# Expert weights of a mixture-of-experts block streamed into a mix of 8 KB and 4 KB slots, with four more tiles of on-chip memory

## The chip, the cores and the metric

The kernel runs on one core of a Trainium2 chip. The metric is the device time of one execution in microseconds; of several executions the median counts. A profile of one further execution, with its own time, shows what each engine did.

## What is computed

One decoder layer on 256 tokens of 1024 channels: four token mixers, merged by gates, then a mixture of 32 experts, each with 256 hidden channels, with a normalisation after either half. The change touches the second half, of which this is the core:

```python
def one_seq(xs):                      # xs: 256 x 1024
    lg = (xs @ wr_g) + br_g           # 4 groups, the best one is taken
    ...                               # two of its eight experts, weights in gate (256 x 32)
    hg = jnp.einsum('sd,edh->seh', xs, w_gate)   # w_gate, w_up: 32 x 1024 x 256
    hu = jnp.einsum('sd,edh->seh', xs, w_up)
    h = jax.nn.silu(hg) * hu * gate[..., None]
    return jnp.einsum('seh,ehd->sd', h, w_down)  # w_down: 32 x 256 x 1024
```

The weights of one expert are three matrices of 1 MiB, so all experts together are 96 MiB. Every expert's weights are read, whichever tokens chose it.

## The kernel before, in words

**The two halves.** The token mixers run first. Their work is written as generators (`gen_S`, `gen_P`, `gen_D` and so on), and the string `ORDER` says, letter by letter, which of them goes on next; so each engine's order of work is written out by hand. The mixers' weights come as loads of 512 KiB (128 partitions with 1024 floats each) into tiles of the pool `rp`, which has `NW` = 35 such tiles. Mixer activations share these tiles.

**The experts' weights.** The list `stream` (L1219) holds all expert loads in the order of use. Experts are worked on in eight groups of four. For each group there are 8 loads of `mwg` (the gate matrices), 8 of `mwu` (up) and 8 of `mwd` (down); each is half of one expert's matrix, 512 KiB, and for each matrix the first halves of all four experts stand ahead of the second halves. The down matrices of the last two groups come last. `fetch()` (L1229) takes the next load of the list, takes a tile for it and issues the DMA on SP's queue. Of 46 loads in a row, 13 go to tiles of the pool `rb` (`NR`, opened when the mixers' own memory is given back) and 33 to tiles of `rp` (`NF`). The letter `L` in `ORDER` calls `fetch()` 46 times (`NL`) while the mixers still run. After that `wload()` (L1253) calls it for each tile that is needed; since SP has its own queue, a load goes out as soon as the tile that it reuses is free and SP has come to it. SP issues in order: a load that waits holds back all loads behind it. Every load also waits until the load eight places ahead of it on SP has landed, since eight semaphores are used in turn.

**The work on a group** (loop at L1518). `gather` (L1429) picks the tokens of the four experts by a matrix product. For `mwg`, then for `mwu`, the loop at L1523 goes over the eight blocks of 128 channels and, inside, over the four experts; each product has 32 columns, and the four experts take four separate column groups of the array (L1527). A product of float32 runs in two passes, so 32 products are 64 rows of the trace. Then follow the activation (L1547 to L1549), two transposes (L1552), the down products (L1496), and `back` (L1514), which adds the result to the tokens. For the last two groups the down products stand behind the loop (L1617 on); their last eight 512 KiB loads are issued as sixteen halves (L1242), and `last_back` (L1642), the statistics and the output follow.

The loop for more tokens than an expert has room for (L1683 on) is not entered with these inputs.

Of the kernel before, what the change touches and what calls it, by code (L numbers as in the profile page):

```python
# [9 lines left out]
F32 = mybir.dt.float32  # L10
# [103 lines left out]
def _layout(inp):  # L114
    g = {k: np.asarray(v) for k, v in inp.items()}
    x = g["x"][0]
    W = g["w_in"][0]
    f = np.float32
    o = {}
# [23 lines left out]
    o["win"] = np.stack(cols)  # L143
    o["wbr"] = g["w_branch"][0].reshape(4, 2, P, 2, 512).transpose(0, 3, 2, 1, 4)
    o["wout"] = g["w_out"][0].reshape(KT, P, D)
    o["mwg"] = g["moe_w_gate"][0].reshape(NEXP, 2, 4, P, HID).transpose(0, 1, 3, 2, 4)
    o["mwu"] = g["moe_w_up"][0].reshape(NEXP, 2, 4, P, HID).transpose(0, 1, 3, 2, 4)
    o["mwd"] = g["moe_w_down"][0].reshape(NEXP, 2, P, D)
    pc = np.zeros((P, NPC), f)

    def put(name, a):
# [21 lines left out]
    for h in range(4):  # L173
        j = 64 * (h % 2)
# [21 lines left out]
MID = 8  # L196
NEAR = 6

NW = 35
NR = 13  # L200
NF = 33
N2 = 19
N1 = 10
NL = 46
RB = 0
LATE = 2
WARM = 5
# [7 lines left out]
    "ADDSAAADDAAABAAAABADDDDBDDDBBDDBBPDBBSDBSBBBBBBDDPDDBBBPCBCBPCSBBCBASPCLCMMCCCCCDMNCMCMCPCCSCCNCPSCP"  # L215
    "PSCPMMNPSPSMPCNMMMCCCDMNPPMSMPSMPSNPMCXLLMLLLLLLLPSPSPSPMPSPPSLPNNMLLMLLLSPMSLMLPSPLPSMPSPMNNPMLPSPS"
    "MMMPSMPSMNNMMMLMMPLMPSPSUMMPMMPMUUSUMUPMMUMPMMMPOUOLMLLLLMLULLUOULLLULMOUULULLMOUUOUUOQOQLQQQQQQQQLQ"
    "QYYLQQUQQQQORLOLLLRLRQRRLRQRRQRRRRQRRRZQZQERRRRRRRLRREQEEQRRE"
)


def body(ctx, tc, I, out):
    nc = tc.nc
    V, A, G, T, SY = nc.vector, nc.scalar, nc.gpsimd, nc.tensor, nc.sync
# [5 lines left out]
    rp = ctx.enter_context(tc.tile_pool(name="rp", bufs=NW))  # L230

    def view(t, n, shape):
        t = t[0:shape[0], 0:n]
        if len(shape) == 2:
            return t
        d = "abcde"[:len(shape) - 1]
        return t.rearrange("p (%s) -> p %s" % (" ".join(d), " ".join(d)), **dict(zip(d, shape[1:])))

    def slot(name, shape, pool=None, dt=F32):

        t = (pool or rp).tile([P, 1024], dt, tag="w", name=name)
        return view(t, int(np.prod(shape[1:])), shape)
# [963 lines left out]
    MP = {}  # L1206
# [12 lines left out]
    stream = []  # L1219
    for g in range(NQUAD + 1):  # L1220
        if g < NQUAD:
            stream += [(src, (4 * g + e, kh), [P, 4, HID]) for src in ("mwg", "mwu") for kh in range(2) for e in range(4)]

        if g != NQUAD - 2:
            for j in ((NQUAD - 2, NQUAD - 1) if g == NQUAD else (g,) if g < NQUAD - 2 else ()):
                stream += [("mwd", (4 * j + e, k), [P, D]) for k in range(2) for e in range(4)]
    fetched, tails = [], []

    def fetch():  # L1229
        n = len(fetched)  # L1230
        src, (e, k), shape = stream[n]
        t = slot("w", shape, MP["rb"] if RB <= n % (NR + NF) < RB + NR else rp)
        fetched.append(t)
        if n < len(stream) - 8:
            SY.dma_start(t, I[src][e][k])
            return

        tails.append((t, I[src][e][k]))
        if n == len(stream) - 1:
            for hs in (slice(0, 512), slice(512, 1024)):  # L1240
                for t, a in tails:
                    SY.dma_start(t[:, hs], a[:, hs])  # L1242
# [245 lines left out]
    outs, wds = {}, {}  # L1488

    def downs(g):  # L1490
        wds[g] = [[wload() for _ in range(4)] for k in range(2)]
        return [ps([P, 512], pj) for _ in range(2)]

    def down(g, k, h, pd):
        for e4 in range(4):
            T.matmul(pd[h][32 * e4:32 * e4 + 32], lhsT=outs[g][0][:, k, 32 * e4:32 * e4 + 32], rhs=wds[g][k][e4][:, 512 * h:512 * h + 512],  # L1496
                     start=k == 0, stop=k == 1, tile_position=(0, 32 * e4))

    def small(shape):
# [18 lines left out]
    for g in range(NQUAD):  # L1518
        xg = XG.pop(g)
        weights(g)  # L1520
        more = g + 1 < NQUAD
        pgu = ps([P, 2, HID])
        for i, src in enumerate(("mwg", "mwu")):  # L1523
            ws = [[wload() for _ in range(4)] for kh in range(2)]
            for k in range(KT):
                for e4 in range(4):
                    T.matmul(pgu[32 * e4:32 * e4 + 32, i], lhsT=xg[:, k, 32 * e4:32 * e4 + 32], rhs=ws[k // 4][e4][:, k % 4, :],  # L1527
                             start=k == 0, stop=k == KT - 1, tile_position=(0, 32 * e4))
            if i == 0:
# [38 lines left out]
        if g < NQUAD - 2:  # L1568
            pd = downs(g)
# [65 lines left out]
    g = NQUAD - 1  # L1635
# [15 lines left out]
    pd = downs(g)  # L1651
# [31 lines left out]
    with tc.If(flag > 0):  # L1683
# [13 lines left out]
        with tc.For_i(0, NEXP, 1) as e:  # L1697
            wg, wu, wd_ = ([slot("wo", sh) for _ in range(2)] for sh in ([P, 4, HID], [P, 4, HID], [P, D]))
            for i in range(2):
                SY.dma_start(wg[i], I["mwg"][bass.ds(e, 1)][0, i])  # L1700
                SY.dma_start(wu[i], I["mwu"][bass.ds(e, 1)][0, i])
                SY.dma_start(wd_[i], I["mwd"][bass.ds(e, 1)][0, i])
            hx = slot("hx", [P, 2, S])
            pg = ps([P, 2, S])
            pu2 = ps([P, 2, S])
# [42 lines left out]
```

## Time and profile before

| | |
|---|---|
| median of 3 executions | 513.37 us (512.88 to 514.83) |
| the profiled execution, its own time | 511.94 us |
| its span, first to last instruction | 510.2 us |
| mean granted TensorE clock | 0.981 |
| PE busy | 467.2 us (92%) |
| DVE, ACT, POOL busy | 241.7, 195.8, 47.0 us |
| moved by DMA | 146.82 MB |

The profiled execution took 1.7 us more than its span; it is 1.4 us under the median. "Busy" counts the time in which at least one instruction of the engine was under way. PE is TensorE, PEld its weight loads, DVE VectorE, ACT ScalarE, POOL GpSimd, SP the engine that issues DMAs. Idle time is put down to what ended it. The span can be read in three stretches: the mixers until about 290 us, the routing of tokens until 299.5 us, and the experts from there on.

### The profile page before, as it was taken

Reading aid. Unit: us, or ns where it says so; the run is one execution under the profiler, and the core shown is the slowest. Engines: PE = TensorE matmul, PEld = TensorE weight load, DVE = VectorE, ACT = ScalarE, POOL = GpSimd, SP = SyncE. Lnnn points to the kernel's source line nnn. Section 1 sums busy time; section 2 is a strip of 40 time slices with the busy share of each in tenths; the row PEclk is TensorE's granted clock in tenths of the full one; section 3 lists DMA queues with packets and bytes.
Section 4 is the critical chain, followed back from the end, with each engine's and each line's share of the span. In section 5 each row is a group of like instructions: output and inputs, shape, how many; then the busy total and the mean of one; then the engine's idle time right before and its main releaser. Section 6 shows DMA issues by size and latency. Waiting matters only on the chain. (4 is left out here: it accounts for less than half of the span.)

```text
span 510.2 us, 10633 instructions
## 1 busy us (share of the span) xinstructions
PE 467.2 (92%) x4396; PEld 357.0 (70%) x4396; DVE 241.7 (47%) x479; ACT 195.8 (38%) x357; POOL 47.0 (9%) x55
## 2 busy tenths in 40 slices
PE   8999999999999999999999899998898989777891
PEld 6888887998778999999998676554453635343420
DVE  4786659987868558544764643021111211111015
ACT  5967555366494465434353342020201201001311
POOL 2003022300000012123150000000000000000002
PEclk9999999999999999999999989999999999989896
DMA  8999432212332452999879869999999999999962
GB/s 283 350 371 383 141 110 84 89 39 84 123 127 84 145 187 90 408 410 409 336 288 413 287 242 406 407 409 408 409 408 408 409 409 409 408 410 408 401 239 84
DMA packets 44410, 146.82 MB, mean 288 GB/s; under 512 B 4996, under 2 KB 7624, under 8 KB 44360
## 3 DMA queue, kind: packets, MB, share of 16 engines
q1 hardware_dynamic: 44360, 146.12, 75.0%
q8 instruction: 35, 0.57, 0.4%
q14 instruction: 15, 0.12, 0.1%
HBM read 143.48 MB, written 2.62 MB: 286 GB/s over the span
## 5 line engine op out<-in xcount | busy, mean ns | idle before, releaser
L374 PE MATMUL ps<-xl,hi 128*128 128x256 f32 x416 | 122.3, 294 | 1.9 <-DVE vS L385 1.1
L375 PE MATMUL ps<-xh,lo 128*128 128x256 f32 x416 | 118.0, 284 | 0.4 <-DVE lo L360 0.3
L376 PE MATMUL ps<-xh,hi 128*128 128x256 f32 x416 | 117.6, 283 | 0.0
L360 DVE TENSOR_TENSOR lo<-w,hi 128x1024 fp32r<-128x1024 f32 (+1 forms) x75 | 89.1, 1206 | 53.1 <-ACT hi L359 45.5
L374 PEld LDWEIGHTS ps<-xl,hi 128*128 128x128 f32 x416 | 79.7, 192 | 5.6 <-issue 1.9
L375 PEld LDWEIGHTS ps<-xh,lo 128*128 128x128 f32 x416 | 79.7, 192 | 2.6 <-issue 1.4
L359 ACT CAST hi<-w 128x1024 fp32r<-128x1024 f32 (+1 forms) x75 | 74.2, 1014 | 16.9 <-PE ps L375 5.1
L376 PEld LDWEIGHTS ps<-xh,hi 128*128 128x128 f32 x416 | 79.7, 192 | 0.0
L1527 PE MATMUL ps<-w,xg 128*32 128x256 f32 x1024 | 69.0, 393 | 7.8 <-DMA w<-mwu 7.0
L1527 PEld LDWEIGHTS ps<-w,xg 128*32 128x32 f32 x1024 | 34.0, 112 | 39.7 <-DMA w<-mwu 12.2
L1429 PE MATMUL ps<-Sel,nrm 128*128 128x128 f32 x256 | 33.6, 286 | 1.3 <-DVE smr L1395 0.7
L1429 PEld LDWEIGHTS ps<-Sel,nrm 128*128 128x128 f32 x256 | 31.3, 200 | 4.8 <-issue 4.1
L1514 PE MATMUL ps<-small,SGT 128*128 128x512 f32 x48 | 23.7, 616 | 9.1 <-DVE small L1508 5.1
L1508 DVE COPY small<-ps 128x512 f32<-128x512 f32 x6 | 4.2, 692 | 53.2 <-PE ps L1514 53.2
L1479 ACT COPY SGT<-ps 128x256 f32<-128x256 f32 x8 | 3.0, 373 | 65.8 <-PE ps L1477 65.8
L1496 PE MATMUL ps<-w,small 128*32 128x512 f32 x192 | 24.7, 599 | 3.7 <-ACT xg L1436 3.0
L1514 PEld LDWEIGHTS ps<-small,SGT 128*128 128x128 f32 x48 | 8.2, 189 | 24.9 <-DVE small L1508 10.1
L1669 POOL TENSOR_TENSOR res<-res,ln 128x512 f32<-128x512 f32 x1 | 1.7, 1730 | 239.2 <-ACT res L1668 239.2
L1422 DVE TENSOR_TENSOR Sel<-rank,csts 128x128 f32<-128x128 f32 x16 | 4.0, 288 | 32.7 <-PE ps L1477 32.7
L374 PE MATMUL ps<-parts,hi 128*128 128x256 f32 x64 | 18.8, 293 | 0.0
L1496 PEld LDWEIGHTS ps<-w,small 128*32 128x32 f32 x192 | 5.4, 109 | 18.3 <-ACT xg L1436 7.5
L375 PE MATMUL ps<-parts,lo 128*128 128x256 f32 x64 | 18.1, 283 | 0.0
(417 smaller groups left out, 703.2 us busy)
## 6 DMA issues: line engine op xcount, KB each, us to landing
w<-mwg SPq DMA_DIRECT2D x64, 512.0 KB, 10.2
w<-mwu SPq DMA_DIRECT2D x64, 512.0 KB, 10.2
w<-mwd SPq DMA_DIRECT2D x56, 512.0 KB, 10.2
w<-win SPq DMA_DIRECT2D x54, 512.0 KB, 5.4
w<-wbr SPq DMA_DIRECT2D x8, 512.0 KB, 4.1
w<-wout SPq DMA_DIRECT2D x8, 512.0 KB, 7.9
w<-mwd SPq DMA_DIRECT2D x16, 256.0 KB, 5.3
scr<-fsb SPq DMA_DIRECT2D x1, 1536.0 KB, 7.0
```

The lines of the kernel that those rows point to most:

```text
L359: A.copy(hi, src)
L360: V.tensor_tensor(lo, src, hi.bitcast(F32), op=OP.subtract)
L374: T.matmul(dst, lhsT=ls[0], rhs=rs[1], start=start, stop=False)
L375: T.matmul(dst, lhsT=ls[1], rhs=rs[0], start=False, stop=False)
L376: T.matmul(dst, lhsT=ls[0], rhs=rs[0], start=False, stop=stop)
L1422: V.tensor_tensor(t, rank[q][:, 4 * g:4 * g + 4, None].broadcast_to([P, 4, 32]), C("iota")[:, None, :].broadcast_to([P, 4, 32]), op=OP.is_ ...
L1429: T.matmul(pg[:, k4], lhsT=nrm[q][:, 128 * k:128 * k + 128], rhs=f2(SelR[g, q]), start=q == 0 and k4 == 0, stop=True, skip_group_check=True)
L1479: A.copy(SGT, pg)
L1496: T.matmul(pd[h][32 * e4:32 * e4 + 32], lhsT=outs[g][0][:, k, 32 * e4:32 * e4 + 32], rhs=wds[g][k][e4][:, 512 * h:512 * h + 512], start=k ...
L1508: V.tensor_copy(dn[h], pd[h])
L1514: T.matmul(yacc[q, h], lhsT=outs[g][1][:, q], rhs=dn[h], start=False, stop=False, skip_group_check=True)
L1527: T.matmul(pgu[32 * e4:32 * e4 + 32, i], lhsT=xg[:, k, 32 * e4:32 * e4 + 32], rhs=ws[k // 4][e4][:, k % 4, :], start=k == 0, stop=k == KT ...
```

## The change

Four things change together.

- The three expert matrices are laid out in memory so that one expert's matrix is one piece of 8 KB per partition, in place of two matrices of 4 KB per partition.
- `stream` lists whole matrices, expert by expert (96 entries). Of 25 entries in a row, the first 7 go to the pool `rb`, whose 7 tiles now hold 8 KB per partition: one DMA of 1 MiB fills one. The other 18 go to `rp` as two loads of 512 KiB into two tiles; each of these now reads 4 KB out of every 8 KB.
- The DMA scratch area is set to 256 bytes per partition. `rp` gets 38 tiles in place of 35, `rb` the room of 14 in place of 13. `NL` is 50 in place of 46, and four letters `L` stand at the end of `ORDER`.
- The last eight matrices are issued in blocks of four experts, first halves ahead of second halves, so that they come in the order they had before.

```diff
-    o["mwg"] = g["moe_w_gate"][0].reshape(NEXP, 2, 4, P, HID).transpose(0, 1, 3, 2, 4)
-    o["mwu"] = g["moe_w_up"][0].reshape(NEXP, 2, 4, P, HID).transpose(0, 1, 3, 2, 4)
-    o["mwd"] = g["moe_w_down"][0].reshape(NEXP, 2, P, D)
+    o["mwg"] = g["moe_w_gate"][0].reshape(NEXP, KT, P, HID).transpose(0, 2, 1, 3)
+    o["mwu"] = g["moe_w_up"][0].reshape(NEXP, KT, P, HID).transpose(0, 2, 1, 3)
+    o["mwd"] = g["moe_w_down"][0].reshape(NEXP, 2, P, D).transpose(0, 2, 1, 3)
...
-NW = 35
-NR = 13
-NF = 33
+NW = 38
+NR = 7
+NF = 36
...
-NL = 46
+NL = 50
...
-    "QYYLQQUQQQQORLOLLLRLRQRRLRQRRQRRRRQRRRZQZQERRRRRRRLRREQEEQRRE"
+    "QYYLQQUQQQQORLOLLLRLRQRRLRQRRQRRRRQRRRZQZQERRRRRRRLRREQEEQRRELLLL"
...
-            stream += [(src, (4 * g + e, kh), [P, 4, HID]) for src in ("mwg", "mwu") for kh in range(2) for e in range(4)]
+            stream += [(src, 4 * g + e, [P, KT, HID]) for src in ("mwg", "mwu") for e in range(4)]
...
-                stream += [("mwd", (4 * j + e, k), [P, D]) for k in range(2) for e in range(4)]
+                stream += [("mwd", 4 * j + e, [P, 2, D]) for e in range(4)]
...
-        n = len(fetched)
-        src, (e, k), shape = stream[n]
-        t = slot("w", shape, MP["rb"] if RB <= n % (NR + NF) < RB + NR else rp)
-        fetched.append(t)
+        n, half = len(fetched) // 2, len(fetched) % 2
+        src, e, shape = stream[n]
+        m = shape[1] // 2
+        if n % (NR + NF // 2) < NR:
+            if half:
+                fetched.append(fetched[-1])
+                return
+            t = view(MP["rb"].tile([P, 2048], F32, tag="w2", name="w2"), 2048, shape)
+            at, a = (lambda k: t[:, k]), I[src][e]
+        else:
+            t = slot("w", [shape[0], m, shape[2]])
+            at, a = (lambda k: t[:, k - m * half]), I[src][e][:, m * half:m * half + m]
+        fetched.append(at)
         if n < len(stream) - 8:
-            SY.dma_start(t, I[src][e][k])
+            SY.dma_start(t, a)
             return
...
-            ws = [[wload() for _ in range(4)] for kh in range(2)]
+            ws = [wload() for _ in range(4)]
             for k in range(KT):
                 for e4 in range(4):
-                    T.matmul(pgu[32 * e4:32 * e4 + 32, i], lhsT=xg[:, k, 32 * e4:32 * e4 + 32], rhs=ws[k // 4][e4][:, k % 4, :],
+                    T.matmul(pgu[32 * e4:32 * e4 + 32, i], lhsT=xg[:, k, 32 * e4:32 * e4 + 32], rhs=ws[e4](k),
...
-    nc = _bacc.Bacc("TRN2", target_bir_lowering=False, num_devices=1)
+    nc = _bacc.Bacc("TRN2", target_bir_lowering=False, num_devices=1, dynamic_dma_scratch_size=256)
```

PE, ACT, DVE and POOL keep every instruction in its place; only SP's order differs. In the built programs a row of SP names the tile that a DMA fills (`w_` a 4 KB tile, `w2_` an 8 KB tile), its source, its size in floats per partition, and the semaphores that it waits for (`DMAHW0` to `DMAHW7` are those of earlier DMAs).

The first place is the end of the loads ahead of the experts' work and the first refills. Before, `w_3675` is the 46th and last load that needs no finished expert work:

```order
L1235 DMA w_3601<-mwd 128x1024 [waits DMAHW1_49,PE_49]
L1235 DMA w_3609<-mwd 128x1024 [waits DMAHW2_49,PE_49]
L1235 DMA w_3675<-mwd 128x1024 [waits DMAHW3_49,Activation_49]
L1235 DMA w_4012<-mwd 128x1024 [waits DMAHW4_49,PE_49]
L1235 DMA w_4014<-mwd 128x1024 [waits DMAHW5_49,PE_49]
L1235 DMA w_4054<-mwg 128x1024 [waits DMAHW6_49,PE_49]
L1235 DMA w_4056<-mwg 128x1024 [waits DMAHW7_49,PE_49]
```

After the change, the same stretch of SP:

```order
L1245 DMA w_3587<-mwd 128x1024 [waits DMAHW2_49,PE_49]
L1245 DMA w_3595<-mwd 128x1024 [waits DMAHW3_49,Activation_49]
L1245 DMA w_3661<-mwd 128x1024 [waits DMAHW4_49,PE_49]
L1245 DMA w_3707<-mwd 128x1024 [waits DMAHW5_49,PE_49]
L1245 DMA w_3709<-mwd 128x1024 [waits DMAHW6_49]
L1245 DMA w_3711<-mwg 128x1024 [waits DMAHW7_49,PE_49,Activation_49]
L1245 DMA w_3713<-mwg 128x1024 [waits DMAHW0_49,Activation_49]
L1245 DMA w2_4044<-mwg 128x2048 [waits DMAHW1_49,PE_49]
L1245 DMA w2_4046<-mwg 128x2048 [waits DMAHW2_49,PE_49]
L1245 DMA w2_4048<-mwg 128x2048 [waits DMAHW3_49,PE_49]
L1245 DMA w2_4091<-mwu 128x2048 [waits DMAHW4_49,PE_49]
```

Four more loads (`w_3707` to `w_3713`) stand ahead of the first refill, and `w_3713` waits for the step of ACT for which `w_3675` waited before. The first refill is now a 1 MiB load into an 8 KB tile; it waits for the last product of the first group's gate loop, where `w_4012` waited for the end of that loop's first half.

The second place is SP at the turn from the seventh group to the eighth and last. Before:

```order
L1235 DMA w_4863<-mwu 128x1024 [waits DMAHW4_49,PE_49]
L1235 DMA w_4865<-mwu 128x1024 [waits DMAHW5_49,PE_49]
L1235 DMA w_4937<-mwg 128x1024 [waits DMAHW6_49,PE_49]
L1235 DMA w_4939<-mwg 128x1024 [waits DMAHW7_49,PE_49]
L1235 DMA w_4941<-mwg 128x1024 [waits DMAHW0_49,PE_49]
```

After:

```order
L1245 DMA w2_4811<-mwu 128x2048 [waits DMAHW2_49,PE_49]
L1245 DMA w2_4813<-mwu 128x2048 [waits DMAHW3_49,PE_49]
L1245 DMA w2_4885<-mwg 128x2048 [waits DMAHW4_49,PE_49]
L1245 DMA w2_4887<-mwg 128x2048 [waits DMAHW5_49,PE_49]
L1245 DMA w_4889<-mwg 128x1024 [waits DMAHW6_49]
L1245 DMA w_4891<-mwg 128x1024 [waits DMAHW7_49]
```

The up matrices of the seventh group and two gate matrices of the last come whole; all loads behind them are halves, the first and the second half of one expert one after the other.

## Rows read from the trace of the kernel before

**Rows 1.** Page, the span in 40 slices of 12.75 us: busy tenths of PE; GB/s.

```profile
PE   8999999999999999999999899998898989777891
GB/s 283 350 371 383 141 110 84 89 39 84 123 127 84 145 187 90 408 410 409 336 288 413 287 242 406 407 409 408 409 408 408 409 409 409 408 410 408 401 239 84
```

**Rows 2.** Stretches: length, busy PE, PEld, DVE, ACT, POOL, clock, DMA share, GB/s.

```profile
200.00:280.00 80.00, 80.00 (x599) 76.95 (x598) 44.28 (x45) 34.41 (x42) 16.66 (x13) 1.00 0.95 372
300.00:304.00 4.00, 4.00 (x74) 2.22 (x70) 2.39 (x15) 2.18 (x9) 0.00 (x0) 1.00 0.38 121
310.00:470.00 160.00, 140.50 (x1393) 74.82 (x1391) 27.14 (x80) 21.21 (x53) 0.00 (x0) 0.99 1.03 409
481.00:484.00 3.00, 3.00 (x28) 3.00 (x28) 0.00 (x0) 1.39 (x3) 0.00 (x0) 1.00 1.04 389
485.00:490.00 5.00, 5.00 (x24) 1.70 (x16) 0.69 (x1) 0.85 (x2) 0.00 (x0) 1.00 0.97 349
```

**Rows 3.** What SP's queue waited for: total us, times, longest.

```profile
SPq L1235 <- DMA w<-mwu: 44.5, 50, 1.3
SPq L1235 <- DMA w<-mwg: 42.7, 50, 1.2
SPq L1235 <- PE ps L1527: 15.4, 12, 7.0
```

**Rows 4.** Timeline of SP around the first refills: start, us, what, count.

```profile
294.20 0.33 SPq L1235 DMA_DIRECT2D w<-mwd  x1
...
301.47 1.68 SPq L1235 DMA_DIRECT2D w<-mwd  x2
...
303.24 4.88 SPq L1235 DMA_DIRECT2D w<-mwg  x8
```

**Rows 5.** Timeline of PE, first, third and fourth group.

```profile
299.53 3.66 PE L1527 MATMUL ps<-w,xg 128*32 128x256 f32 x64
303.12 0.44 PE L1477 MATMUL ps<-csts,Sel 128*128 128x128 f32 x2
...
351.56 3.66 PE L1527 MATMUL ps<-w,xg 128*32 128x256 f32 x64
...
373.12 3.66 PE L1527 MATMUL ps<-w,xg 128*32 128x256 f32 x64
```

**Rows 6.** Timeline of PE, last group's up matrices and the end.

```profile
468.46 1.92 PE L1527 MATMUL ps<-w,xg 128*32 128x256 f32 x28 [0.66 <-DMA w<-mwu]
...
473.58 3.52 PE L1527 MATMUL ps<-w,xg 128*32 128x256 f32 x26 [0.66 <-DMA w<-mwu]
478.57 0.41 PE L1552 MATMUL ps<-csts,hh 128*128 128x128 f32 x2 [1.47 <-DVE hh L1549]
...
493.19 1.99 PE L1642 MATMUL ps<-dn,SGT 128*128 128x512 f32 x4
495.10 1.06 PE L1496 MATMUL ps<-w,hh 128*32 128x512 f32 x8
```

**Rows 7.** Issues of the last loads on SP, and median us from issue to landing.

```profile
484.23 5.63 SPq L1242 DMA_DIRECT2D w<-mwd  x9
...
w<-mwu SPq DMA_DIRECT2D x64, 512.0 KB, 10.2
...
w<-mwd SPq DMA_DIRECT2D x16, 256.0 KB, 5.3
```

**Rows 8.** DMA queues: packets, MB, share.

```profile
q1 hardware_dynamic: 44360, 146.12, 75.0%
q8 instruction: 35, 0.57, 0.4%
```

**Rows 9.** Timeline of ACT: casts of mixer weights, and the gate that reads their product.

```profile
216.92 1.99 ACT L359 CAST hi<-w 128x1024 fp32r<-128x1024 f32 x2
...
230.22 0.59 ACT L476 ACTIVATE gC<-ps 128x512 f32<-128x512 f32 x1
```

**Rows 10.** Stretches as in rows 2: the granted clock late in the last two groups.

```profile
457.00:473.00 16.00, 12.91 (x137) 7.31 (x135) 2.67 (x8) 2.25 (x6) 0.00 (x0) 1.00 1.03 409
473.80:477.10 3.30, 3.29 (x26) 1.22 (x18) 0.00 (x0) 0.00 (x0) 0.00 (x0) 0.50 1.03 410
```

More of the change, by code (lines that the diff above doesn't have):

```diff
@@ L1221, in body @@
         if g < NQUAD:
-            stream += [(src, (4 * g + e, kh), [P, 4, HID]) for src in ("mwg", "mwu") for kh in range(2) for e in range(4)]
+            stream += [(src, 4 * g + e, [P, KT, HID]) for src in ("mwg", "mwu") for e in range(4)]
         if g != NQUAD - 2:
             for j in ((NQUAD - 2, NQUAD - 1) if g == NQUAD else (g,) if g < NQUAD - 2 else ()):
-                stream += [("mwd", (4 * j + e, k), [P, D]) for k in range(2) for e in range(4)]
+                stream += [("mwd", 4 * j + e, [P, 2, D]) for e in range(4)]
     fetched, tails = [], []
     def fetch():
-        n = len(fetched)
-        src, (e, k), shape = stream[n]
-        t = slot("w", shape, MP["rb"] if RB <= n % (NR + NF) < RB + NR else rp)
-        fetched.append(t)
+        n, half = len(fetched) // 2, len(fetched) % 2
[11 more added lines that the diff above has]
+        fetched.append(at)
         if n < len(stream) - 8:
-            SY.dma_start(t, I[src][e][k])
+            SY.dma_start(t, a)
             return
[L1238 to L1242, printed above, removed]
+        whole = n % (NR + NF // 2) < NR
+        tails.extend((k, at(k), I[src][e][:, k]) for k in ((0, 1) if whole else (half,)))
+        if n % 4 == 3 and (half or whole):
+            for hs in (slice(0, 512), slice(512, 1024)) if n == len(stream) - 1 else (slice(0, 1024),):
+                for _, d, b in sorted(tails, key=lambda x: x[0]):
+                    SY.dma_start(d[:, hs], b[:, hs])
+            tails.clear()
     def gen_L():
@@ L1253, in wload @@
     def wload():
-        if used[0] == len(fetched):
+        while len(fetched) < 2 * used[0] + 2:
             fetch()
+        lo, hi = fetched[2 * used[0]:2 * used[0] + 2]
+        m = stream[used[0]][2][1] // 2
         used[0] += 1
-        return fetched[used[0] - 1]
+        return lambda k: lo(k) if k < m else hi(k)
     po = {}
@@ L1490, in downs @@
     def downs(g):
-        wds[g] = [[wload() for _ in range(4)] for k in range(2)]
+        wds[g] = [wload() for _ in range(4)]
         return [ps([P, 512], pj) for _ in range(2)]
@@ L1495, in down @@
         for e4 in range(4):
-            T.matmul(pd[h][32 * e4:32 * e4 + 32], lhsT=outs[g][0][:, k, 32 * e4:32 * e4 + 32], rhs=wds[g][k][e4][:, 512 * h:512 * h + 512],
+            T.matmul(pd[h][32 * e4:32 * e4 + 32], lhsT=outs[g][0][:, k, 32 * e4:32 * e4 + 32], rhs=wds[g][e4](k)[:, 512 * h:512 * h + 512],
                      start=k == 0, stop=k == 1, tile_position=(0, 32 * e4))
@@ L1699, in body @@
             for i in range(2):
-                SY.dma_start(wg[i], I["mwg"][bass.ds(e, 1)][0, i])
-                SY.dma_start(wu[i], I["mwu"][bass.ds(e, 1)][0, i])
-                SY.dma_start(wd_[i], I["mwd"][bass.ds(e, 1)][0, i])
+                SY.dma_start(wg[i], I["mwg"][bass.ds(e, 1)][0, :, 4 * i:4 * i + 4])
+                SY.dma_start(wu[i], I["mwu"][bass.ds(e, 1)][0, :, 4 * i:4 * i + 4])
+                SY.dma_start(wd_[i], I["mwd"][bass.ds(e, 1)][0, :, i])
             hx = slot("hx", [P, 2, S])
```

## The prediction

> **What bounds the kernel now.** I read the slices first. PE is busy almost without a break up to 290 us, and the DMA engines move 400 GB/s and more from about 204 us on, with dips up to 319 us and none from there to 485 us [rows 1]. So there are two bounds, one behind the other, and the stretches show the turn: from 200 to 280 us PE is busy for 80.00 of 80 us, from 310 to 470 us it idles for 19.5 us while the DMA runs at 409 GB/s [rows 2]. At that rate a load of 512 KiB (0.524 MB) takes 1.282 us. Next I read what SP waits for. In the experts' half nearly every load waits for the landing of an earlier one, about 1 us at a time, and only 15.4 us are waits for expert products [rows 3]. So for most of that half there are free tiles, and eight loads are always in flight: the transfer itself is the limit.
>
> The end of the kernel therefore hangs on when the unbroken stream begins and on how much is left to stream at that moment. The begin is seen on SP: the 46th load goes out at 294.20 us and the next two at 301.47 us [rows 4], and between 300 and 304 us the DMA moves 121 GB/s [rows 2]. All tiles are full, and the first comes free when PE has gone through the first half of the first gate loop, which began at 299.53 us [rows 5]. PE needs 373.12 - 351.56 = 21.6 us for a group when it has its data [rows 5], against 24 x 1.282 = 30.8 us for a group's loads, so PE catches up with the stream. In the last group it waits for every single up matrix, the last one until 473.58 us [rows 6]. What follows is a chain of PE, ACT and DVE work.
>
> At the very end two things are about equally late. The last 256 KB load is issued at 484.23 + 5.63 - 0.33 = 489.53 us and lands 5.3 us later [rows 7], at 494.8 us. The products that need it start at 495.10 us, straight behind PE's work before them [rows 6]. So a shift of the stream moves both, and PE's chain alone could gain only 0.3 us more than the stream.
>
> **The change, part by part.**
>
> *Four more tiles.* 50 half loads in place of 46 stand ahead of the first refill, and the last of them waits for the same ACT step as the 46th did. That load was issued at 294.20 us [rows 4], with about 7 us to spare, in which the four fit (5.1 us). Four loads fewer are left for the stream: -4 x 1.282 = **-5.1 us**. If they did not go out in that time, the term would be 0.
>
> *The first refill comes later.* An 8 KB tile is free only when the whole gate loop has read it. The loop's 64 passes started at 299.53 us and PE's next work at 303.12 us [rows 5]; with the step to SP I take 303.2 us in place of 301.47 us. The DMA has nothing to do then, so all of it counts: **+1.7 us**. From there it does not dry up: the seven 8 KB tiles of the first group come free within the gate and up loops, about 4 us each, and hold 18 us of transfers.
>
> *Rows of 8 KB.* Behind the first refill, up to the last up matrix, 130 half loads stood before; now it is 126, of which 42 are in 21 whole loads. Their price is not in the trace, so I take it from two row sizes. With rows of 4 KB the 16 DMA engines move 409 GB/s, with rows of 2 KB 389 GB/s while the queue was full (481 to 484 us) [rows 2]. A row of 4 KB then takes an engine 16 x 4096 B / 409 GB/s = 160.2 ns, one of 2 KB 84.2 ns; what does not grow with the size is 2 x 84.2 - 160.2 = 8.2 ns. A row of 8 KB spares one of these, 2.6% of 320 ns: 42 x 1.282 x 0.026 = **-1.4 us**. The bounds are 0, if a long row is moved like two of 4 KB, and -2.7 us, if this doubling brought as much as the one from 2 to 4 KB (5%). [...]
>
> *Expert by expert.* [...] Now the fourth expert's first half is the seventh of eight loads, and nearly all passes, 58, stand behind it, 1.28 us ahead of the last landing. At the full clock 28 passes took 1.92 us [rows 6], about 0.054 us a pass and 0.4 us for the last one's way; at half the clock a pass takes twice that. The 58 would take 3.5 us at the full clock, 6.7 us at half, and 5.2 us with 3.4 us of it at half and the rest at full, since here too the half clock held from the burst's start to 477.1 us [rows 10]. Less 1.28 us this is 2.2, 5.4 or 3.9 us behind the last landing, against 3.5 us before: -1.3, +1.9 or **+0.4 us**; I take the last, since the clock behaved so. The seventh group, whose up matrices come whole, has about as much more to do after its last landing, but the eighth group's data come so late that PE waits again afterwards; I cost that at nothing.
>
> *The rest.* SP issues 28 loads fewer, which costs nothing, since it waits anyway [rows 3]. No queue but the hardware one and the instruction fetch carries packets [rows 8], so the small scratch area costs nothing. The five mixer loads behind the first expert loads now queue behind 5 MiB in place of 4.5 MiB and land up to 1.3 us later; casts at about 217 us and the gate at 230.22 us [rows 9] lie far enough apart to cover that. Were that cover gone, it would cost PE at most those 1.3 us. Tiles that come free earlier in the mixers gain nothing where PE is already busy all the time.
>
> The sum is -5.1 + 1.7 - 1.4 + 0.4 = **-4.4 us**. The profiled execution of 511.94 us would become 507.5 us; the median of the runs lies 1.4 us above it, so 513.37 us becomes **509.0 us**.
>
> **The rivals.**
>
> *Less is gained.* Long rows bring nothing and PE goes through the last up loop at half clock all the way: -5.1 + 1.7 + 1.9 = -1.5 us, 511.9 us. [...]
>
> *More is gained.* From 301.47 to 473.5 us 130 loads took 172 us, but 130 x 1.282 is 166.7 us. The other 5.4 us are the first load's way and losses that no row names. If they go by the number of loads (105 in place of 130), 1.0 us more goes, and the up loop at full clock would give up to 1.7 us, of which the last landing lets 0.3 + 0.4 through: -6.1 us, 507.3 us.
>
> *It doesn't do what it says.* If SP reaches the four extra loads only behind a wait that the rows don't show, they go out with the refills: 0 + 1.7 - 1.4 + 0.4 = +0.7 us, 514.1 us. Against it: they wait for nothing that ends after 294.2 us.
>
> *Slower.* The half loads now read 4 KB out of every 8 KB. If the memory served such pieces more slowly, every one of them would pay: 84 up to the last up matrix and 16 behind it, 100 x 1.282 = 128 us of stream. From a rate 3.4% lower on, the gain of 4.4 us is gone. The lowest rate of a busy stretch, 349 GB/s for 2 KB out of every 4 KB [rows 2], would give 128 x (409 / 349 - 1) = +22 us, so 531 us. Against it: the same kind of pieces ran at 389 GB/s just before, which the row size alone could explain. [...]
>
> **How the numbers follow.** About 0.5%, 2.6 us, is what a measurement of this kernel can tell from no change. The forecast (-2.7 to -5.5 us) gets 0.58, more gained 0.12, less gained 0.18, the change that doesn't do what it says 0.07, slower 0.05. Less gained lies on either side of -2.6 us: 0.07 of it counts as faster, 0.11 as same. Faster is 0.58 + 0.12 + 0.07 = 0.77; same 0.11 + 0.06 = 0.17; slower 0.05 + 0.01 = 0.06. The range reaches from a little below the case of more (506.2 us) to a little above the case of less (512.4 us); the two cases above it and the tails are left out.
>
> **What would show it.** SP's timeline should have 50 half loads (7 whole ones among them) out by 295 us, the next at about 303.2 us, with a deeper hole in GB/s around 300 us. The last wait for `mwu` should end at about 468.7 us, with 58 passes behind the wait before it. The whole loads should show over 409 GB/s where they stand alone, about 420. The last products should again start right behind the last landing, near 490.7 us. The forecast is wrong if the stream has gaps behind 304 us, if its rate falls under 409 GB/s, or if PE's end no longer follows the stream.

## The result, and the profile after

The changed kernel takes 508.81 us (median of 12 runs, 504.66 to 512.70), the kernel before 514.78 us in 12 runs beside them (512.46 to 517.45). The ratio is 0.9873, 95% interval [0.9843, 0.9903], so 5.0 to 8.1 us less. Forecast were 509.0 us and a gain of 4.4 us: the time is the forecast one, the gain is larger, because the kernel before took 514.78 us in these runs and 513.37 us in those from which the forecast was counted. The profiled execution took 506.87 us with a span of 505.0 us; the one before had a span of 510.2 us, 5.2 us more.

The page of the changed kernel (the span, then PE's busy tenths and GB/s in 40 slices, now 12.6 us long, and the packets):

```profile
span 505.0 us, 10569 instructions
...
PE   8999999999989999999999989998988989867891
...
GB/s 286 363 365 396 172 114 45 124 3 92 119 133 78 167 168 36 421 415 409 408 257 411 394 251 366 394 412 409 408 418 414 409 410 408 421 414 408 399 226 85
DMA packets 40377, 146.81 MB, mean 291 GB/s; under 512 B 4548, under 2 KB 7176, under 8 KB 36744
```

Against [rows 1] slices of 414 to 421 GB/s have appeared beside those of 408 to 410. The 24th slice, around 300 us, moves the least of the weight stream, 251 GB/s (242 before); that the hole there is deeper than before shows only in the stretches. Stretches of the changed kernel (columns as in [rows 2]):

```profile
300.00:304.00 4.00, 4.00 (x74) 2.22 (x70) 2.35 (x15) 2.13 (x9) 0.00 (x0) 1.00 0.01 4
310.00:470.00 160.00, 138.07 (x1392) 74.97 (x1394) 27.12 (x80) 21.17 (x53) 0.00 (x0) 0.97 1.02 411
...
320.00:324.00 4.00, 4.00 (x27) 3.04 (x26) 0.00 (x0) 0.00 (x0) 0.00 (x0) 1.00 0.98 353
322.00:324.00 2.00, 2.00 (x15) 1.52 (x14) 0.00 (x0) 0.00 (x0) 0.00 (x0) 1.00 0.92 270
410.00:420.00 10.00, 8.32 (x82) 3.53 (x74) 1.09 (x3) 0.58 (x1) 0.00 (x0) 1.00 1.03 408
430.00:440.00 10.00, 8.32 (x76) 3.41 (x68) 1.09 (x3) 0.58 (x1) 0.00 (x0) 1.00 1.02 421
...
488.00:489.00 1.00, 1.00 (x6) 0.49 (x3) 0.00 (x0) 0.14 (x1) 0.00 (x0) 1.00 0.15 57
489.00:490.00 1.00, 1.00 (x3) 0.19 (x1) 0.64 (x1) 0.00 (x0) 0.00 (x0) 1.00 0.00 0
```

The transfers stand still from 300 to 304 us (121 GB/s before, [rows 2]). Half loads stream at 408 GB/s (410 to 420 us), whole ones at 421 (430 to 440 us). At 320 to 324 us the stream has a dent, 353 GB/s, with 270 from 322 us on. The last bytes arrive at about 488.7 us (494.2 us before).

SP at the first refill, and PE at the first gate loop, in the last up loop and at the end (start, us, what, count, idle time before):

```profile
303.15 1.28 SPq L1245 DMA_DIRECT2D w<-mwg  x3
304.52 3.90 SPq L1245 DMA_DIRECT2D w<-mwu  x4
316.42 8.10 SPq L1245 DMA_DIRECT2D w<-mwd  x8
```

```profile
299.48 3.66 PE L1542 MATMUL ps<-w,xg 128*32 128x256 f32 x64
...
464.78 0.62 PE L1542 MATMUL ps<-w,xg 128*32 128x256 f32 x2 [1.87 <-DMA w<-mwu]
467.35 5.17 PE L1542 MATMUL ps<-w,xg 128*32 128x256 f32 x58 [1.95 <-DMA w<-mwu]
473.99 0.41 PE L1567 MATMUL ps<-csts,hh 128*128 128x128 f32 x2 [1.48 <-DVE hh L1564]
474.33 1.92 PE L1511 MATMUL ps<-w,hh 128*32 128x512 f32 x16
...
488.20 1.98 PE L1657 MATMUL ps<-dn,SGT 128*128 128x512 f32 x4
490.11 1.06 PE L1511 MATMUL ps<-w,hh 128*32 128x512 f32 x8
```

The first refill went out 3.67 us behind the start of the first gate loop (1.94 us before, [rows 4, 5]). Behind the seven whole loads the next ones, halves, go out from 316.42 us on. Fifty-eight passes stand behind the last wait for `mwu` and take 5.17 us, as predicted; the last products start at 490.11 us (495.10 before, [rows 6]).

### The profile page after: what moved, and what is told of

Read it like the earlier page. It is cut to its first block, busy times and chain, and to the rows that moved or that the text cites. A ratio compares the mean times of both kernels' runs of the same rounds, so it can differ in the third digit from the quotient of the medians.

```text
span 505.0 us, 10569 instructions
## 1 busy us (share of the span) xinstructions
PE 461.7 (91%) x4396; PEld 356.8 (71%) x4396; DVE 244.7 (48%) x479; ACT 195.2 (39%) x357; POOL 47.7 (9%) x55
## 5 line engine op out<-in xcount | busy, mean ns | idle before, releaser
L360 DVE TENSOR_TENSOR lo<-w,hi 128x1024 fp32r<-128x1024 f32 (+1 forms) x75 | 90.8, 1232 | 44.1 <-ACT hi L359 43.4
L1542 PE MATMUL ps<-w,xg 128*32 128x256 f32 x1024 | 65.7, 400 | 8.4 <-DMA w<-mwu 8.4
L1511 PE MATMUL ps<-w,small 128*32 128x512 f32 x192 | 23.1, 598 | 3.5 <-ACT xg L1451 3.0
L374 PE MATMUL ps<-parts,hi 128*128 128x256 f32 x64 | 18.8, 294 | 0.0
L376 PE MATMUL ps<-parts,hi 128*128 128x256 f32 x64 | 18.1, 283 | 0.0
```

Source lines behind the costliest of these rows:

```text
L360: V.tensor_tensor(lo, src, hi.bitcast(F32), op=OP.subtract)
L374: T.matmul(dst, lhsT=ls[0], rhs=rs[1], start=start, stop=False)
L376: T.matmul(dst, lhsT=ls[0], rhs=rs[0], start=False, stop=stop)
```

## The experiments

**A measure for single profiles.** In the profiled executions of the table the first gate loop of the experts begins anywhere from 298.9 to 306.3 us, and TensorE's granted clock ahead of it differs: 0.50 from 293 to 296 us in the kernel before and in the changed kernel, 0.50 from 300 to 306 us in the profile that begins at 306.3 us, and 1.00 from 280 to 300 us in the one that begins at 298.9 us. No row ties that to the expert loads, so I measure each profile from the start of that loop to the start of the last products, two rows of PE's timeline. The kernel before gives 495.10 - 299.53 = 195.57 us, and with the small scratch area, which changes nothing else, 195.62 us.

| kernel | first gate loop, us | last products, us | between | against before | ratio of the runs |
|---|---|---|---|---|---|
| before | 299.53 | 495.10 | 195.57 | | |
| small scratch alone | 299.80 | 495.42 | 195.62 | +0.05 | 1.0005 [0.9978, 1.0033] |
| four tiles alone | 300.25 | 490.38 | 190.13 | -5.44 | 0.9926 [0.9887, 0.9965] |
| four tiles alone, again | 302.80 | 494.02 | 191.22 | -4.35 | 0.9949 [0.9917, 0.998] |
| layout and 8 KB slots alone | 300.93 | 496.55 | 195.62 | +0.05 | 1.0032 [1.0009, 1.0055] |
| the change | 299.48 | 490.11 | 190.63 | -4.94 | 0.9873 [0.9843, 0.9903] |
| change, whole loads cut by rows | 299.97 | 493.65 | 193.68 | -1.89 | 0.9957 [0.993, 0.9983] |
| change, 8 KB rows cut, loads whole | 306.34 | 499.45 | 193.11 | -2.46 | 0.9974 [0.9942, 1.0007] |
| change, last group's first halves first | 300.57 | 490.56 | 189.99 | -5.58 | 0.9886 [0.984, 0.9933] |
| change, half slots refilled first | 298.92 | 496.01 | 197.09 | +1.52 | 1.007 [1.0038, 1.0102] |
| the last two together | 299.89 | 497.61 | 197.72 | +2.15 | 1.0033 [0.9997, 1.0068] |
| change, first group expert by expert | 301.16 | 508.04 | 206.88 | +11.31 | 1.0211 [1.0155, 1.0267] |
| that, last group's first halves first | 299.97 | 505.93 | 205.96 | +10.39 | 1.0174 [1.0121, 1.0227] |

The kernel before had a median of 514.78 us beside the changed kernel and of 512.68 to 513.49 us beside the experiments, so ratios of different rows may differ by 0.2 to 0.4% for that alone.

### The parts of the change

The scratch area alone: `_bacc.Bacc(..., dynamic_dma_scratch_size=256)` in the kernel before.

> The kernel before with the DMA scratch area at 256 bytes and nothing else. Theory: no queue uses the area, so no change: within 0.5 us of before, span about 510, first refill at 301.5 us, last wait for an up matrix until about 473.5 us. Rival (the area matters to a transfer, or the place of the tiles does): 1 us or more in either direction, with the rate of the stream off 409 GB/s.

Measured: 513.52 us beside 513.49 us. Within 0.3% the small area by itself costs and gains nothing; the next kernel has four more tiles with it.

Four more tiles, with 4 KB rows, half loads and the order as before:

```diff
-NW = 35
-NR = 13
-NF = 33
+NW = 38
+NR = 14
+NF = 36
...
-NL = 46
+NL = 50
...
-    "QYYLQQUQQQQORLOLLLRLRQRRLRQRRQRRRRQRRRZQZQERRRRRRRLRREQEEQRRE"
+    "QYYLQQUQQQQORLOLLLRLRQRRLRQRRQRRRRQRRRZQZQERRRRRRRLRREQEEQRRELLLL"
...
-    nc = _bacc.Bacc("TRN2", target_bir_lowering=False, num_devices=1)
+    nc = _bacc.Bacc("TRN2", target_bir_lowering=False, num_devices=1, dynamic_dma_scratch_size=256)
```

> The kernel before with the small scratch area and four more 4 KB tiles (50 loads ahead in place of 46); layout, order of loads and rows of 4 KB as before. Theory: four loads fewer are left when the stream begins, and the first refill stays at about 301.5 us: -5.1 us against before, last wait for an up matrix until about 468.4 us, span about 505.1 us. By the theory this is 0.7 us better than the change itself. Rival (the gain of the change comes from the long rows and whole loads, not from tiles): no gain here, 0 to -1 us.

Measured: 509.68 us. PE's timeline in the last up loop and at the end:

```profile
469.18 1.91 PE L1527 MATMUL ps<-w,xg 128*32 128x256 f32 x26 [0.66 <-DMA w<-mwu]
472.57 0.41 PE L1552 MATMUL ps<-csts,hh 128*128 128x128 f32 x2 [1.48 <-DVE hh L1549]
...
474.30 1.90 PE L1496 MATMUL ps<-w,hh 128*32 128x512 f32 x10 [0.23 <-DMA w<-mwd]
...
490.38 1.06 PE L1496 MATMUL ps<-w,hh 128*32 128x512 f32 x8
```

The last wait for `mwu` ends 4.4 us earlier than before [rows 6]; counted from the start of the first gate loop it is 168.93 us against 174.05 us, 5.1 us earlier, as the theory has it. The span is 505.4 us against 510.2 us. So in this profile the tiles give the whole gain without the layout; in the runs they give 0.74%, where the change gives 1.27%. Here the clock stayed up (1.00 from 469 to 472 us, 26 passes in 1.91 us; before 0.50, 3.52 us, [rows 6, 10]), and PE then waits for `mwd`, which it did not in the changed kernel: the loads are now the later of the two ends.

The layout and the 8 KB slots without the four tiles:

```diff
-NW = 38
-NR = 7
-NF = 36
+NW = 36
+NR = 6
+NF = 34
...
-NL = 50
+NL = 46
...
-    "QYYLQQUQQQQORLOLLLRLRQRRLRQRRQRRRRQRRRZQZQERRRRRRRLRREQEEQRRELLLL"
+    "QYYLQQUQQQQORLOLLLRLRQRRLRQRRQRRRRQRRRZQZQERRRRRRRLRREQEEQRRE"
```

> The change without its four tiles: the expert layout in one piece, 6 slots of 8 KB and 34 of 4 KB, 46 half loads ahead, small scratch area. Theory: first refill late (+1.7 us), 18 whole loads on the stream (-1.2 us), expert by expert (+0.4 us): +0.9 us against before, so about the same; first refill at 303.2 us, last wait for an up matrix until about 473 us less 1.3 us. Rival (long rows carry the gain): -3 to -5 us.

Measured: 514.64 us, 1.6 us above before (0.5 to 2.8), span 511.8 us. The layout alone gains nothing; the rival that lets long rows carry the gain falls.

By these profiles the layout on top of the four tiles is worth between -0.6 us (190.63 against 191.22) and +0.5 us (against 190.13). The ratios say more: 0.9873 with it, 0.9926 and 0.9949 without. I ran the tiles a second time for this:

> The kernel before with the four more tiles alone, a second time. Its profiled execution was as short as the changed kernel's (from the first expert product to the last products 190.13 us, against 190.63 us in the changed kernel and 195.57 us before), but its median gave a ratio of 0.9926 [0.9887, 0.9965] against 0.9873 [0.9843, 0.9903] of the changed kernel. Theory (the four tiles carry all of the gain, 5.4 us): ratio 0.988 to 0.991, the same stretch again 189.8 to 190.5 us. Rival (the long rows add half a per cent that the one profile does not show): ratio 0.992 to 0.994.

Measured: 510.56 us, and 191.22 us between the two rows. The ratio fits neither: it lies above the theory's 0.988 to 0.991 and just above the rival's 0.992 to 0.994. The medians themselves, 509.68 and 510.56 us against 508.81 us, leave 0.9 to 1.8 us for the layout; the rest of the difference in the ratios lies in the medians of the kernel before. That the tiles alone gain is shown, and that the layout alone does not. How the gain divides is not shown: by the profiles the tiles carry all of it, by the ratios 0.51% and 0.74% of 1.27%. Whether the layout adds some microseconds to them or nothing, stays open.

### What a long row and a whole load are worth

Each 1 MiB load cut into two half loads with 4 KB rows, which fill the halves of the same slot:

```diff
-            SY.dma_start(t, a)
+            if shape[1] == t.shape[1]:
+                SY.dma_start(t[:, 0:m], a[:, 0:m])
+                SY.dma_start(t[:, m:2 * m], a[:, m:2 * m])
+            else:
+                SY.dma_start(t, a)
```

> The change with each 1 MiB load cut into two of 512 KiB with rows of 4 KB into the two halves of the same 8 KB slot. Theory: only the saving of the long rows goes: +1.4 us against the change, so about -4.6 us against before by the measured -6.0 of the change; the rate of the stream is 409 GB/s throughout, where the change shows up to 421. Rival 1 (long rows save nothing): no difference to the change. Rival 2 (whole loads save more than their rows, by fewer issues or fewer loads in flight): +3 us or more.

Measured: 512.03 us, and 3.05 us more between the two rows than in the changed kernel, where 1.4 were expected; of the three cases the second rival's, whole loads that save more than their rows, comes nearest. The stretches of this kernel:

```profile
304.00:306.00 2.00, 2.00 (x40) 1.23 (x44) 0.42 (x2) 0.37 (x1) 0.00 (x0) 1.00 0.67 219
306.00:308.00 2.00, 2.00 (x36) 1.16 (x29) 0.00 (x0) 0.27 (x1) 0.00 (x0) 1.00 0.92 330
308.00:310.00 2.00, 2.00 (x21) 2.00 (x20) 1.23 (x4) 0.29 (x2) 0.00 (x0) 1.00 0.65 186
...
330.00:470.00 140.00, 120.85 (x1259) 63.58 (x1258) 22.97 (x71) 19.09 (x48) 0.00 (x0) 0.97 1.03 409
```

and the same of the changed kernel:

```profile
304.00:306.00 2.00, 2.00 (x44) 1.20 (x40) 0.00 (x0) 0.00 (x0) 0.00 (x0) 1.00 0.83 270
306.00:308.00 2.00, 2.00 (x31) 1.36 (x21) 0.34 (x1) 0.38 (x1) 0.00 (x0) 1.00 0.98 414
308.00:310.00 2.00, 2.00 (x20) 2.00 (x19) 1.38 (x5) 0.37 (x1) 0.00 (x0) 1.00 1.04 438
...
330.00:470.00 140.00, 120.17 (x1286) 64.64 (x1282) 22.97 (x71) 19.08 (x48) 0.00 (x0) 0.97 1.02 412
```

Most of the 3 us is in two parts: a steady 409 against 412 GB/s, 1.0 us over 140 us, and a dip of the rate right behind the first refill, which the whole loads don't have. From 304 to 312 us 0.88 MB less are moved, of which 0.20 MB go with the start of the refill, here 0.49 us later (303.64 us); the rest is 1.7 us. Two kernels were to tell the row's length from the size of the load. The first cut each whole load by partitions, 64 each, so that the rows stay 8 KB long (`t[0:64], a[0:64]` and `t[64:128], a[64:128]` in the diff above):

> The changed kernel with each 1 MiB load cut in two by partitions (64 partitions each), so that the rows stay 8 KB long and only the loads become 512 KB. The kernel with 4 KB rows in the same slots had a span of 508.7 us against 505.0, of which about 2.2 us are a dip of the rate just after the first refill (219, 330, 186, 363 GB/s in the four stretches of 2 us from 304 us, against 270, 414, 438, 418) and about 1.1 us the steady rate (409 against 412 GB/s from 330 to 470 us). Theory (the steady rate is the row's, the dip is the half load's): 1 MiB per pair of loads at 411 to 412 GB/s from 330 to 470 us, the dip comes back, span about 507.2. Rival 1 (all of it is the row's length): no dip, span 504.5 to 505.5. Rival 2 (all of it is the number of loads): 409 GB/s and the dip, span about 508.7. A load on 64 partitions could also be slower by itself, which would show below 409 GB/s.

Measured: 574.48 us, ratio 1.1175 [1.1122, 1.1227]. The case that the text names last came, and much more strongly than meant. Two stretches of this kernel, the first with loads on 64 partitions under way, the second with loads on 128:

```profile
330.00:340.00 10.00, 9.63 (x64) 6.01 (x65) 0.22 (x1) 0.59 (x1) 0.00 (x0) 1.00 1.02 216
...
360.00:370.00 10.00, 8.32 (x82) 3.71 (x74) 1.89 (x9) 0.59 (x1) 0.00 (x0) 1.00 1.02 407
```

A load on half of the partitions moves at about half the rate, 216 GB/s against 407, with the DMA engines' busy share at 1.02 in both; why, no run shows. The kernel therefore says nothing of the row's length. The second one left 8 bytes free in the middle of each slot, so that a whole load stays one load but its rows become two pieces of 4 KB:

```diff
-            t = view(MP["rb"].tile([P, 2048], F32, tag="w2", name="w2"), 2048, shape)
-            at, a = (lambda k: t[:, k]), I[src][e]
+            t = MP["rb"].tile([P, 2, 1026], F32, tag="w2", name="w2")[:, :, 0:1024]
+            t = t.rearrange("p h (m c) -> p h m c", m=m)
+            at, a = (lambda k: t[:, 0, k] if isinstance(k, slice) else t[:, k // m, k % m]), I[src][e].rearrange("p (h m) c -> p h m c", h=2)
...
```

> The changed kernel with 8 bytes left free in the middle of each 8 KB slot (scratch 192 bytes), so that each 1 MiB load stays one load but its rows become two pieces of 4 KB. Together with the kernel that had two 512 KB loads into halves of the slot (span 508.7, 3.7 us over the changed kernel: about 2.2 us of a dip in the rate after the first refill, about 1.1 us of steady rate) it parts the row's length from the size of the load. Theory (steady rate from the row's length, dip from the size of the load): 409 GB/s from 330 to 470 us, no dip between 306 and 316 us, span 505.8 to 506.5. Rival 1 (all from the row's length): 409 GB/s and the dip, span about 508.7. Rival 2 (all from the size of the load): 411 to 412 GB/s, no dip, span 504.7 to 505.3.

Measured: 511.08 us. In the profile the clock was 0.82 from 280 to 290 us, 0.67 from 290 to 300 us and 0.50 from 300 to 306 us; the first gate loop began at 306.34 us and the first refill went out at 310.29 us. Its stretches:

```profile
312.00:314.00 2.00, 2.00 (x44) 1.03 (x35) 0.00 (x0) 0.00 (x0) 0.00 (x0) 1.00 0.95 336
314.00:316.00 2.00, 2.00 (x23) 1.85 (x17) 0.84 (x2) 0.38 (x1) 0.00 (x0) 1.00 0.99 401
330.00:470.00 140.00, 123.19 (x1273) 65.56 (x1272) 24.06 (x74) 18.71 (x47) 0.00 (x0) 0.98 1.03 409
```

Both marks of the theory are there: with pieces of 4 KB the steady rate is 409 GB/s, so the row's length sets it; and 4 to 6 us behind the refill the rate is 401 GB/s, so the dip belongs to the half loads. The 2.5 us more between the two rows are above the 0.8 to 1.5 us of the theory: 1.0 is that rate, and 1.2 is a slower last up loop (58 passes in 6.33 us, from 475.52 us on; the clock was 0.71 from 470 to 480 us, in the changed kernel over the same distances from its last wait 0.83). The runs agree that long rows pay in the changed kernel: with the rows cut the ratio is 0.9974 [0.9942, 1.0007] against 0.9873 [0.9843, 0.9903]. Why half loads dip where a dried-up stream begins again, no run shows.

This kernel bears on the changed kernel's dent at 322 to 324 us, too. SP waits nearly as long for the down products behind the seven whole loads (7.4 us, in the changed kernel 8.0 us), yet with rows of 4 KB no stretch of 2 us from 316 to 332 us is under 399 GB/s. So that wait alone does not make the dent.

### The order of the last loads

The last group's eight up halves, all first halves first as before the change:

```diff
-        if n < len(stream) - 8:
+        if n < len(stream) - 12:
             SY.dma_start(t, a)
+            return
+        if n < len(stream) - 8:
+            ups.append((half, t, a))
+            if n % 4 == 3 and half:
+                for _, d, s in sorted(ups, key=lambda x: x[0]):
+                    SY.dma_start(d, s)
```

> The changed kernel with one thing put back: the eight half loads of the last group's up matrices are issued all first halves first, as before the change. Theory: the waits on the up loads in the last group become about 0.65 us instead of 1.9, 26 to 28 passes instead of 58 stand behind the last landing (1.9 us or less instead of 5.2), TensorE's granted clock does not fall to 0.5 there; the last transfers end at about 488.1 us all the same and the last products follow them by 1.1 us instead of 2.0, so the span is shorter by 0.9 us (about 504.1; bounds -0.3 to -1.9). Rival (the order of the halves is worth nothing, the last loads set the end): span 504.8 to 505.2. Rival (the recorded term with its lower bound): longer by up to 1.3 us.

Measured: 507.25 us, not to be told from the changed kernel. PE's timeline:

```profile
468.29 0.62 PE L1548 MATMUL ps<-w,xg 128*32 128x256 f32 x2 [0.66 <-DMA w<-mwu]
469.57 1.91 PE L1548 MATMUL ps<-w,xg 128*32 128x256 f32 x26 [0.66 <-DMA w<-mwu]
...
474.70 1.90 PE L1517 MATMUL ps<-w,hh 128*32 128x512 f32 x10 [0.24 <-DMA w<-mwd]
...
490.56 1.07 PE L1517 MATMUL ps<-w,hh 128*32 128x512 f32 x8
```

The waits are 0.66 us, 26 passes are left and run at the full clock. They take 3.3 us less than the 58 passes of the changed kernel but start 1.1 us later behind the first gate loop (169.00 against 167.87 us), so the loop ends 2.1 us earlier. PE then waits for `mwd`, and only 0.64 us reach the end (189.99 against 190.63). The clock in the same stretch of the two kernels, first this one, then the changed kernel:

```profile
466.00:469.00 3.00, 1.63 (x8) 0.27 (x4) 0.00 (x0) 0.00 (x0) 0.00 (x0) 1.00 1.02 408
469.00:472.00 3.00, 1.91 (x26) 0.90 (x26) 0.06 (x1) 0.38 (x1) 0.00 (x0) 1.00 1.03 410
```

```profile
466.00:469.00 3.00, 1.65 (x16) 0.79 (x20) 0.00 (x0) 0.00 (x0) 0.00 (x0) 0.68 1.02 408
469.00:472.00 3.00, 3.00 (x45) 1.57 (x38) 0.00 (x0) 0.00 (x0) 0.00 (x0) 0.75 1.02 407
```

With waits of 0.66 us the clock stayed at 1.00 here, with waits of 1.87 and 1.95 us it was 0.50 from 468 to 470 us. The length of the waits alone does not decide it: in the kernel before the waits are 0.64 to 0.66 us as well, and its last 26 passes ran at 0.50 and took 3.52 us [rows 6, 10].

### An earlier first refill

The 8 KB slots given to the entries 4 to 10 of each 25 and fetched first, so that the slots that come free first are 4 KB ones:

```diff
+    seq = list(range(4, 11)) + list(range(4)) + list(range(11, len(stream)))
...
-        n, half = len(fetched) // 2, len(fetched) % 2
+        i, half = len(fetched) // 2, len(fetched) % 2
+        n = seq[i]
+        whole = 4 <= n % (NR + NF // 2) < 4 + NR
...
```

> The changed kernel with the 8 KB slots given to the entries 4 to 10 of each 25 and those fetched first, then the entries 0 to 3 as half loads, so that the first slot that comes free is a 4 KB one. Theory (the transfers run until the end, so a first refill 1.7 us earlier ends them 1.7 us earlier): first refill at about 301.5 us instead of 303.15, last transfer at about 486.4 instead of 488.1, span about 503.3. Rival (the half loads at the first refill bring back the dip of the rate that the kernel with 4 KB rows has there, 2.2 us): span 505.0 to 505.5, no gain. Rival (the hole at 300 us is worth nothing): span 505.0.

Measured: 516.75 us, worse than before the change. SP's timeline, its longest wait, and stretches of this kernel:

```profile
300.90 3.69 SPq L1248 DMA_DIRECT2D w<-mwg  x6
315.93 3.65 SPq L1248 DMA_DIRECT2D w<-mwu  x5
```

```profile
SPq L1248 <- PE ps L1513: 12.6, 2, 11.3
```

```profile
312.00:314.00 2.00, 1.82 (x16) 1.12 (x16) 1.36 (x4) 0.13 (x1) 0.00 (x0) 1.00 0.04 14
314.00:316.00 2.00, 1.53 (x16) 0.50 (x16) 0.66 (x2) 0.00 (x0) 0.00 (x0) 1.00 0.00 0
```

The first refill came early, at 300.90 us, but only six half loads went out. The next one stands in SP's queue for a 4 KB slot that a down product (L1513) frees at 315.9 us, and behind it wait loads whose 8 KB slots the up products had freed long before. The stream stands still for some 4 us. I had counted which slots are free, not which slot the next load in the queue takes. This and the foregoing order together, with the last group's two whole up matrices cut into halves as well:

> Both of the foregoing together: the 8 KB slots at the entries 4 to 10 of each 25, fetched first, and in the last group all first halves of the up matrices first. Theory: -1.7 for the first refill and -0.9 for the last group, span about 502.4, median about 2.6 us under that of the changed kernel (ratio to the kernel before about 0.982). Rival (the dip takes back what the early refill gives): span about 504.1 to 504.6.

Measured: 515.10 us; the same hole (0 GB/s from 314 to 316 us), and 0.6 us more between the two rows, where the order of the halves had saved 0.6.

Then the other way round: the slots as in the change, but the first group's products expert by expert, so that the first 8 KB slot is read through sooner:

```diff
-            for k in range(KT):
-                for e4 in range(4):
+            for n in range(4 * KT):
+                k, e4 = (n % KT, n // KT) if g == 0 else (n // 4, n % 4)
```

(With the loop's body moved one level out.)

> The changed kernel with one thing more: the 64 passes of the first group's gate products and the 64 of its up products run expert by expert (8 per matrix and half) instead of all four experts side by side, so that the first 8 KB slot is free after a quarter of the gate passes. Theory (with the whole loads in flight the stream does not starve again, so the transfers end earlier by as much as the first refill does): first refill at 300.4 us if the passes keep their 57 ns, at about 301.3 if they lose their overlap, against 303.15; last transfer and last products 1.8 to 2.7 us earlier, span 502.3 to 503.2. Rival 1 (the stream stands still between the up products' slots and the down products' slots, which come no earlier, so that the gain is given back in a new hole around 318 to 324 us): span 504.5 to 505.3. Rival 2 (the passes lose their overlap and the later slots come as late or later): span 505 to 507.

Measured: 524.92 us, ratio 1.0211. PE's timeline and SP's:

```profile
301.16 11.50 PE L1542 MATMUL ps<-w,xg 128*32 128x256 f32 x64
```

```profile
304.83 5.57 SPq L1245 DMA_DIRECT2D w<-mwg  x3
312.69 9.51 SPq L1245 DMA_DIRECT2D w<-mwu  x4
333.77 4.16 SPq L1245 DMA_DIRECT2D w<-mwd  x8
```

The 64 passes take 11.50 us, 180 ns each, in place of 3.66 us: the second rival's case, at a price far above its own (a span of 522.9 us where it had 505 to 507 us). The first slot is free no sooner than before, and the down products come 16 us later, so the stream dries up again from 326 to 334 us (23 GB/s). The same with the last group's first halves first:

> The foregoing and the last group's up halves issued first halves first. In the run with the latter alone the last products came 1.3 us behind the last transfer instead of 2.0 us, though its first refill was 1.1 us later by chance. Theory: 0.7 us less than the foregoing, span 501.6 to 502.5, median 2.5 to 3.4 us under the changed kernel (ratio to the kernel before about 0.981). Rival (a hole around 320 us takes the gain of the refill): span 503.8 to 504.6.

Measured: 523.27 us; 0.9 us less between the two rows than without it. No version here is shown to beat the changed kernel; first halves first in the last group saves 0.6 and 0.9 us in two of three pairs of profiles, below what the medians can tell.

## Why the prediction was right, step by step

**The bound.** That the end hangs on when the stream begins and what is left then is what the runs show: the last bytes come at about 488.7 us in place of 494.2 us, the last products 4.99 us earlier. Where the stream was disturbed (half slots first, expert by expert), the time rose with it.

**Four more tiles, -5.1 us.** Alone they gave -5.44 and -4.35 us in two profiles, and the mechanism is the predicted one: in the first of them the last wait for `mwu` ends 5.1 us earlier behind the first gate loop. In the ratios of the runs it was less, -0.74% and -0.51% (3.8 and 2.6 us, each about 1.6 to 2 us uncertain).

**The first refill, +1.7 us.** Measured against the gate loop: 3.67 - 1.94 = 1.73 us. The sentence that from there the stream does not dry up failed in part: at 320 to 324 us it moves 353 GB/s, which is 4 x (411 - 353) / 411 = 0.6 us lost. The seven whole loads are out at 308.4 us and the next ones wait for the down products until 316.42 us, but that is nearly 6 us ahead of the dent, and the kernel with whole loads and cut rows waits nearly as long and has none. Loads are out when the rate falls, and why it falls, no run shows.

**Rows of 8 KB, -1.4 us.** The rates are the predicted ones: 421 GB/s where whole loads stand alone, 408 with half loads, 3.2% where 2.6% was taken. Over 330 to 470 us it makes 412 against 409 GB/s in the two kernels with cut rows and 408 in the kernel before, 1.0 to 1.4 us.

**Expert by expert, +0.4 us.** Fifty-eight passes in 5.17 us, as written, against the 26 in 3.52 us at a clock of 0.50 before [rows 6, 10]. Putting the old order back saved 0.64 us in one pair of profiles and 0.92 us in another, and cost 0.63 us in a third, so the size of the term is not settled. What PE could have saved is far more, but the transfers of `mwd` let no more through.

**What the sum left out.** The kernel before did not stream at its full rate behind its first refill either:

```profile
302.00:304.00 2.00, 2.00 (x38) 0.99 (x34) 1.25 (x6) 0.37 (x1) 0.00 (x0) 1.00 0.73 233
304.00:306.00 2.00, 2.00 (x44) 1.23 (x40) 0.00 (x0) 0.00 (x0) 0.00 (x0) 1.00 0.73 219
```

In the 10 us from 302 us on, with its refill at 301.47 us [rows 4], it moved 3.27 MB, the changed kernel from 304 us on 3.95 MB (five stretches of 2 us each); less 0.13 MB for the refill's distance of 0.53 and 0.85 us, that is 0.55 MB or 1.3 us. It looks like the half loads' dip, but SP also waited a second time for PE there, 0.9 us, at its second refill; no run parts the two. With the measured sizes the sum is -5.1 + 1.7 + 0.6 - 1.0 + 0.6 - 1.3 = -4.5 us, the profiles give -4.94 us. The forecast's -4.4 came near the profiles partly by luck, because two missing terms, +0.6 and -1.3, cancel in part.

In the runs the gain was larger, 5.0 to 8.1 us, and 4.4 us lies below that. That 509.0 us fell so near 508.81 us is luck as well: the kernel before was 1.4 us slower in these runs than in those from which the forecast was counted. What the runs have beyond the profiles' 4.9 us, no trace shows.

**The rivals.** Slower: half loads that read 4 KB out of every 8 KB stream at 408 GB/s; it falls. Doesn't do what it says: the refill came where the extra loads said; it falls. Less gained: the long rows did bring something and the loop was not at half the clock throughout (0.50 from 468 to 470 us, 1.00 from 471 us on); it falls. More gained: by size, -6.1 us, it fits the runs better than the forecast does. Of its reasons, losses that go by the number of loads show at the restart alone, and the last up loop did not run at the full clock (0.70 over its 58 passes).

**What was wrong in "what would show it".** The last products do not start right behind the last bytes any more: these end at about 488.7 us, 1.4 us ahead of the products at 490.11 us (0.9 us before). From its last wait for `mwu`, which ends at 467.35 us, no row has PE wait for a load, so PE's own chain sets the end. The stream is not far ahead of it: where the old order of the last loads let PE end its up loop 2.1 us earlier, 0.64 us reached the end.

## What to carry to other kernels

When a stream of weights at its full rate sets the end, count the bytes that are loaded before it starts and the time at which the first slot comes free; room for four more tiles was worth the whole gain in the profiles and about half of it in the runs, and larger loads without that room gained nothing. Before slots or an order are moved, follow the queue that issues the loads one by one: the slot that the next load takes, not the number of free slots, decides, and everything behind it waits, here up to 11.3 us. Products that run side by side (here 64 passes in 3.66 us) should not be put in a row (11.50 us) to free a buffer sooner.

## What the runs showed of the hardware that was not expected

Two loads in a row onto opposite halves of the partitions do not make up for each other: 216 GB/s against 407, with the DMA engines' busy share at 1.02 in both. Four experts' products on different quarters of TensorE's columns take 57 ns a pass when they alternate (64 in 3.66 us) and 180 ns when one expert's follow each other (64 in 11.50 us).

Half loads dip at a restart of the stream (186 GB/s, 4 to 6 us behind the first refill), whole loads do not (438 GB/s). And the times of one kernel's runs go with the granted clock: of the changed kernel's runs the shortest, 504.66 us, has a mean clock of 0.983, one of 506.87 us has 0.979 and one of 510.26 us 0.973.
